# A second Strassen-like level for M3, and results added to the stored output by accumulating DMAs: an MLP block on one core

## The chip, the cores and the metric

One core of a Trainium2 chip runs the kernel. The metric is the device time in microseconds (us); a kernel's time is the median of several executions. The kernel before repeats within 0.25%.

## The reference, cut to what matters

```python
# x: 8 x 1024 x 1024, w1: 1024 x 4096, w2: 4096 x 1024, all float32
h = x @ w1
h = 0.5 * h * (1 + np.tanh(np.sqrt(2 / np.pi) * (h + 0.044715 * h ** 3)))
return (h @ w2).astype(np.float32)
```

## The kernel before

The kernel works in float16 and takes the 8192 rows in 8 superblocks (numbered from 0) of 1024 rows. Each matrix product is done in the manner of Strassen: the operands are cut into 2 x 2 blocks, and 7 products of sums of blocks replace 8. The first layer (`matmul1`) needs 448 matmuls of 128x512 for a superblock. The second layer (`matmul2`) has products M1 to M7, and its output has four blocks, "11", "12", "21" and "22".

A product at one level is 64 matmuls of 128x512 (13.81 us). A product listed in `INNER` is cut once more in the same manner: 112 matmuls of 128x256 (12.23 us), done by `inner_product`. That saves 1.58 us of TensorE, and costs seven loads of 512 KB in place of four, and more sums. M6 and M7 are inner from superblock 2 on, M1 from superblock 3 on.

A bank is one of the kernel's eight PSUM buffers (`pp`, `bufs=8`) in which TensorE leaves a result; u and d are float32 sums in SBUF, the on-chip memory, from which blocks "11" and "22" are stored; `w_d`, `raw_d` and `in_d` in the tables are operands in DRAM that SyncE loads. Pool is GpSimd.

The parts that matter here:

```python
INNER = (6, 7, 1)
...
up = ctx.enter_context(tc.tile_pool(name="up", bufs=26))   # operands, u and d
tp = ctx.enter_context(tc.tile_pool(name="tp", bufs=10))   # 128x512 float32 temporaries
...
def matmul1(xs, sb, quads):            # first layer: every hidden block takes temporaries
    ...
    for c in range(NI):
        ...
        product(pb, w, 4, True, False)
        v = temp()
        nc.scalar.copy(out=v, in_=pb)
        product(qb, w, 5, True, False)
        u = temp()
        tt(u, v, qb, SUB)              # VectorE
        ...
def matmul2(sb, g, next_x):            # second layer
    ...                                # M4 -> u, inner M1 added to u
    for q, ps in product(2, pb, False):
        c21[q] = temp()
        nc.scalar.copy(out=c21[q], in_=ps)
        store(sb, "21", q, c21[q])
    d2, d = halves()
    x6 = inner_x(6, g)
    xs = next_x()                      # SyncE transposes the next superblock's x
    for q, ps in product(5, qb, True):
        tt(u[q], u[q], ps, SUB)
        tt(d[q], u[q], c21[q], SUB)
    inner_product(6, x6, d2)           # M6 is added to d, in SBUF
    for q, ps in product(3, qb, False):
        c12 = temp()
        nc.scalar.copy(out=c12, in_=ps)
        store(sb, "12", q, c12)
        tt(d[q], d[q], ps, ADD)
        store(sb, "22", q, d[q])
    x7 = inner_x(7, g)
    ...                                # last superblock: results stored from SyncE
    inner_product(7, x7, u2)           # M7 is added to u, in SBUF
    for q in range(NQ):
        last = store(sb, "11", q, u[q])
```

The ten temporaries are shared by the second layer and the first layer of the next superblock. A temporary that is the source of a DMA is free again only when that DMA has landed.

Of the kernel before, what the change touches and what calls it, by code (L numbers as in the profile page):

```python
# [12 lines left out]
ADD = mybir.AluOpType.add  # L13
SUB = mybir.AluOpType.subtract
P = 128
# [32 lines left out]
SUMS = (4, 1, 3, 7, 6)  # L48
PLAIN = (2, 5)
# [3 lines left out]
    {(7, 2): 1, (7, 3): 1, (3, 0): 2, (3, 1): 3, (3, 2): 1, (3, 3): 2, (6, 0): 1, (6, 1): 1, (6, 2): 2, (6, 3): 5},  # L53
)

INNER = (6, 7, 1)
ORDER = (4, 5, 1, 2, 3, 7, 6)


# [1 line left out]
def kernel(  # L61
# [7 lines left out]
    nc = tc.nc  # L69
    x2 = x.flatten_outer_dims()  # L70
    out2 = out.flatten_outer_dims()
# [4 lines left out]
    SB = 1024  # L76
    HT = SB // 2
    NSB = T // SB
    KH = H // P // 2
    NI = I // P // 2  # L80
    OH = O // 2
    NQ = HT // P
# [18 lines left out]
    raw_d = [dram.tile([P, 4, KH * QW], DT, name=f"raw_d{q}") for q in range(NI // QC)]  # L101
    in_d = {m: dram.tile([P, 7, NI // 2, OH // 2], DT, name=f"in_d{m}") for m in INNER}
    w2_d = [dram.tile([P, 7, QC * OH], DT, name=f"w2_d{q}") for q in range(NI // QC)]
# [5 lines left out]
    def temp():  # L109
        return tp.tile([P, HT], F32, name="tmp")  # L110

    def unit(rows, cols):
        return up.tile([P, rows, cols], DT, name="u")

    def tt(out, in0, in1, op, pin=False):
        i = nc.vector.tensor_tensor(out=out, in0=in0, in1=in1, op=op)  # L116
        if pin:
            tc.keep_in_program_order(i)
# [272 lines left out]



    def store(sb, b, q, src):
        r0 = sb * SB + (int(b[0]) - 1) * HT + q * P
        o0 = (int(b[1]) - 1) * OH
        return nc.gpsimd.dma_start(out=out2[r0:r0 + P, o0:o0 + OH], in_=src)  # L397

    def matmul2_made(sb, g, keep_w1, xb):

# [37 lines left out]
        def add(m, q):  # L438
            u, op, v = B_TERMS[m]
            t = sums[m][q]  # L440
            tt(t, raw[u][q], raw[v][q], op, m != 4)
            if sb and m not in INNER[:2]:
                nc.gpsimd.dma_start(out=w2_d[q][:, m - 1, :], in_=flat(t))
# [97 lines left out]
    def split_inner(m, j, pieces):  # L541

        def block(k, b, h):
            return pieces[2 * k + h][:, :, b * OH // 2:(b + 1) * OH // 2]

        u, op, v = B_TERMS[j]
        d = in_d[m][:, j - 1]
        t = None if op is None else unit(NI // 2, OH // 2)
        for h in range(2):
            cs = slice(h * QC, (h + 1) * QC)  # L550
            x0 = block(int(u[0]) - 1, int(u[1]) - 1, h)
            if op is None:
                nc.gpsimd.dma_start(out=d[:, cs, :], in_=x0)
            else:
                tt(t[:, cs, :], x0, block(int(v[0]) - 1, int(v[1]) - 1, h), op, m != 1)
        if op is not None:
            nc.gpsimd.dma_start(out=d, in_=t)

    def inner_x(m, g):

        u, v = A_TERMS[m]
        x = {}
        for b in ("22", "12", "11", "21"):
            a, k = int(b[0]) - 1, int(b[1]) - 1
            at = (slice(None), slice(k * NI // 2, (k + 1) * NI // 2), slice(a * HT // 2, (a + 1) * HT // 2))
            x[b] = unit(NI // 2, HT // 2)
            tt(x[b], g[u][at], g[v][at], SUB)
        return x

    def inner_product(m, x, acc, done=lambda b, t: None):  # L570


        HK, HO = NI // 2, OH // 2
        y = {}
        for j in ORDER:
            y[j] = unit(HK, HO)
            nc.sync.dma_start(out=y[j], in_=in_d[m][:, j - 1])

        def product(j, bank, first):
            u, v = A_TERMS[j]  # L580
            if v is None:
                t = x[u]
            else:
                t = gcp.tile([P, HK, HT // 2], GT, name="gc")
                tt(t, x[u], x[v], SUB)
            for i in range(2):
                for c in range(HK):
                    nc.tensor.matmul(  # L588
                        bank[:, i * HO:(i + 1) * HO],
                        lhsT=t[:, c, i * P:(i + 1) * P],  # L590
                        rhs=y[j][:, c, :],
                        start=(first and i == 0 and c == 0),
                        stop=(c == HK - 1),
                        skip_group_check=not first or i > 0,
                    )

        def part(b):
            a, o = int(b[0]) - 1, int(b[1]) - 1
            return acc[a][:, :, o * HO:(o + 1) * HO]

        def pair(t):
            return t.rearrange("p (i n) -> p i n", i=2)

        pb, qb, rb = psum(), psum(), psum()
        product(4, pb, True)
        v = temp()
        nc.scalar.copy(out=v, in_=pb)
        product(5, qb, True)
        u = temp()
        tt(u, v, qb, SUB)  # L610
        nc.gpsimd.tensor_tensor(out=part("11"), in0=part("11"), in1=pair(u), op=ADD)  # L611
        product(1, rb, True)
        s = temp()
        tt(s, u, rb, ADD)
        product(2, pb, False)
        s2 = temp()
        tt(s2, s, pb, SUB)
        nc.gpsimd.tensor_tensor(out=part("22"), in0=part("22"), in1=pair(s2), op=ADD)

        def add(b, bank):  # L620
            tt(part(b), part(b), pair(bank), ADD)
            done(b, part(b))

        add("21", pb)
        product(3, qb, False)
        s3 = temp()
        nc.scalar.copy(out=s3, in_=qb)
        add("12", s3)
        product(7, rb, False)
        add("11", rb)  # L630
        product(6, qb, False)
        add("22", qb)

    def operand2(g, m, q, pin=False):

# [19 lines left out]
    def product2(g, m, pieces, banks, first, by_chunk=False):  # L655
        if first:
            banks.extend(psum() for _ in range(NQ))
        if by_chunk:
            for c0 in range(0, NI, QC):
                for q in range(NQ):  # L660
                    matmuls2(banks[q], operand2(g, m, q), pieces, first, range(c0, c0 + QC))
                    if c0 + QC == NI:
                        yield q, banks[q]
            return
        for q in range(NQ):
            matmuls2(banks[q], operand2(g, m, q), pieces, first)
            yield q, banks[q]

    def halves():
        tiles = [up.tile([P, 2, OH], F32, name="u") for _ in range(2)]  # L670
        return tiles, [tiles[q // 2][:, q % 2, :] for q in range(NQ)]

    def matmul2(sb, g, next_x):
        def load(m):
            return [load_ops(w2_d[q], raw2_d[q], (m,), QC, OH)[m] for q in range(NI // QC)]

        def product(m, banks, first):
            return product2(g, m, load(m), banks, first)

        c21 = {}  # L680
        pb, qb, rb = [], [], []
        p4 = product(4, pb, True)
        u2, u = halves()
        for q, ps in p4:
            nc.scalar.copy(out=u[q], in_=ps)
        if sb == 2:
            pieces = load(1)
            for q, ps in product2(g, 1, pieces, rb, True):
                tt(u[q], u[q], ps, ADD)
            for j in SUMS + PLAIN:  # L690
                split_inner(1, j, pieces)
        else:
            inner_product(1, inner_x(1, g), u2)
        for q, ps in product(2, pb, False):
            c21[q] = temp()
            nc.scalar.copy(out=c21[q], in_=ps)  # L696
            store(sb, "21", q, c21[q])
        d2, d = halves()
        x6 = inner_x(6, g)
        xs = next_x()  # L700
        for q, ps in product(5, qb, True):
            tt(u[q], u[q], ps, SUB)
            tt(d[q], u[q], c21[q], SUB)
        inner_product(6, x6, d2)
        for q, ps in product(3, qb, False):
            c12 = temp()
            nc.scalar.copy(out=c12, in_=ps)
            store(sb, "12", q, c12)
            tt(d[q], d[q], ps, ADD)
            store(sb, "22", q, d[q])  # L710
        x7 = inner_x(7, g)
        if sb == NSB - 1:

            def store_part(b, t):
                r0, o0 = sb * SB + (int(b[0]) - 1) * HT // 2, (int(b[1]) - 1) * OH // 2
                rows = out2[r0:r0 + HT // 2, o0:o0 + OH // 2]
                nc.sync.dma_start(out=rows.rearrange("(i p) n -> p i n", p=P), in_=t)

            inner_product(7, x7, u2, store_part)
            return None, xs  # L720
        inner_product(7, x7, u2)
        for q in range(NQ):
            last = store(sb, "11", q, u[q])
        return last, xs

    idle = consts.tile([P, HT], DT, name="idle")
    nc.vector.memset(idle, 0.0)
# [3 lines left out]
    xs, quads = x_first(), []  # L731
    for sb in range(NSB):
        g = matmul1(xs, sb, quads)
        if sb < 2:
            xb = x_cast(sb + 1, quads[2].stored) if sb else None
            last, xs, quads = matmul2_made(sb, g, None if sb else quads[-1].keep_raw, xb)
# [6 lines left out]
        last, xs = matmul2(sb, g, next_x)  # L743
# [33 lines left out]
```

## Time and profile before

| | before |
|---|---|
| time | 1548.62 us, median of 4 runs (1548.24 to 1548.99) |
| TensorE busy | 1537.9 of 1548.1 us, 8078 matmuls |
| TensorE waits, the four largest groups, whole run | 1.6, 1.5, 1.2 and 1.1 us |
| granted TensorE clock, mean | 1.00 |
| last matmul to end of the program | 3.9 us (1544.16 to 1548.1) |

The page of the profile, the kernel before: the busy time of each engine (PE is TensorE, PEld its weight load, DVE VectorE, ACT ScalarE, POOL GpSimd), with share of the span and number of instructions; then the DMA queue that Pool issues on (packets, MB, share of the time of all 16 DMA engines).

```profile
PE 1537.9 (99%) x8078; PEld 789.6 (51%) x8078; DVE 1036.4 (67%) x1294; ACT 486.1 (31%) x816; POOL 224.4 (14%) x311
...
q0 software_dynamic: 19440, 74.99, 14.7%
...
out_dram<-tmp POOLq DMA_DIRECT2D x72, 256.0 KB, 5.2
```

The last line is from the table of DMA issues: 72 stores of 256 KB from temporaries, 5.2 us from issue to landing in the median.

The chain of waits in order of time, the kernel before, last superblock (start, duration, engine, tile, line, count):

```profile
1355.52 96.69 PE ps L303 x448
1452.21 13.81 PE ps L646 x64
1466.02 12.23 PE ps L588 x112
1478.25 27.63 PE ps L646 x128
1505.88 12.23 PE ps L588 x112
1518.10 13.81 PE ps L646 x64
1531.92 12.24 PE ps L588 x112
1544.16 0.03 issue
```

This is one superblock read straight off: the first layer, M4, inner M1, M2 with M5, inner M6, M3, inner M7. Each line starts where the last one ended, so TensorE has no gap, and the time of the kernel is the time of its matmuls. Only fewer matmul cycles or new gaps can move it.

### The profile page before, as it was taken

To read this page: it belongs to the slowest core of one execution; us is meant where nothing else is said; L and a number is where in the kernel's file an instruction comes from. 1 tells how busy PE (TensorE), PEld (TensorE's weight loads), DVE (VectorE), ACT (ScalarE), POOL (GpSimd) and SP (SyncE) were. 2 spreads that over 40 slices of the span, in tenths; PEclk is the share of its full clock that TensorE was granted. 3 is DMA by queue.
4 is the path that set the end of the run, shared out by engine and by line. 5 is a ranking of instruction groups with operands and counts; after the bars stand their busy time and mean duration, and the time that the engine had idled before them with its cause. 6 is when DMAs were issued, how large, how long until landed. Compare 5 with 4: busy or idle time off the path is not lost.

```text
span 1548.1 us, 21098 instructions
## 1 busy us (share of the span) xinstructions
PE 1537.9 (99%) x8078; PEld 789.6 (51%) x8078; DVE 1036.4 (67%) x1294; ACT 486.1 (31%) x816; POOL 224.4 (14%) x311
## 2 busy tenths in 40 slices
PE   8999999999999999999999999999999999999998
PEld 4444444444444455445554456544565445744556
DVE  5876868758755666557665677656685567755575
ACT  6655024410244102441034410344113431144301
POOL 1242011112300013001130011200122001200012
PEclk9999999999999999999999999999999999999999
DMA  9999885894992869617795376944769357672553
GB/s 308 345 330 344 250 277 186 284 245 157 348 325 82 238 265 305 266 62 215 277 328 221 110 219 252 354 167 156 233 234 362 117 167 256 251 292 102 189 209 140
DMA packets 169156, 366.30 MB, mean 237 GB/s; under 512 B 73184, under 2 KB 80352, under 8 KB 168160
## 3 DMA queue, kind: packets, MB, share of 16 engines
q1 hardware_dynamic: 149616, 289.98, 54.4%
q0 software_dynamic: 19440, 74.99, 14.7%
q8 instruction: 63, 1.03, 0.3%
q14 instruction: 37, 0.30, 0.1%
HBM read 286.79 MB, written 92.80 MB: 245 GB/s over the span
## 4 chain that ended last, share of the span: by engine, by line
PE 96%; DMA 1%; DVE 1%; ACT 1%; issue 0%; SPq 0%; DVEq 0%; ACTq 0%
PE ps L303 48%; PE ps L646 35%; PE ps L588 13%; DMA gc<-in_w_dram 1%; DVE u L116 1%; DVE tmp L116 0%; ACT g L313 0%; SPq L126 0%; ACT u L191 0%; ACT u L153 0%; ACT u L265 0%; ACT tmp L363 0%; DVEq L116 0%; ACTq L153 0%
## 5 line engine op out<-in xcount | busy, mean ns | idle before, releaser
L303 PE MATMUL ps<-u 128*128 128x512 f16 x3584 | 776.4, 379 | 4.0 <-DVE tmp L116 1.6
L116 DVE TENSOR_TENSOR tmp<-tmp,ps 128x512 f32<-128x512 f32 x579 | 396.2, 686 | 348.6 <-ACT tmp L363 112.8
L303 PEld LDWEIGHTS <-u 128*128 128x128 f16 x3584 | 350.0, 98 | 428.2 <-issue 5.4
L646 PE MATMUL ps<-u,gc 128*128 128x512 f16 x1472 | 319.3, 379 | 0.0
L313 ACT ACTIVATE g<-tmp 128x512 f16<-128x512 f32 x256 | 161.2, 630 | 293.6 <-DVE tmp L116 293.5
L646 PEld LDWEIGHTS <-gc 128*128 128x128 f16 x1472 | 143.7, 98 | 172.9
L646 PE MATMUL ps<-u,g 128*128 128x512 f16 x1024 | 223.6, 379 | 0.0
L313 ACT ACTIVATE g<-ps 128x512 f16<-128x512 f32 x256 | 151.5, 596 | 90.5 <-PE ps L303 90.4
L116 DVE TENSOR_TENSOR u<-u 128x2048 f16<-128x2048 f16 (+2 forms) x164 | 166.1, 1049 | 17.5 <-ACT u L265 12.7
L646 PEld LDWEIGHTS <-g 128*128 128x128 f16 x1024 | 100.0, 98 | 119.7
L588 PE MATMUL ps<-u,gc 128*128 128x256 f16 x1360 | 154.0, 273 | 0.0
L588 PEld LDWEIGHTS <-gc 128*128 128x128 f16 x1360 | 132.9, 98 | 15.6
L116 DVE TENSOR_TENSOR u<-u,ps 128x512 f32<-128x512 f32 x119 | 81.3, 683 | 79.0 <-PE ps L646 47.6
L116 DVE TENSOR_TENSOR gc<-g,g 128x2048 f16<-128x2048 f16 x92 | 117.0, 1284 | 23.4 <-PE ps L646 22.0
L611 POOL TENSOR_TENSOR u<-u,tmp 128x512 f32<-128x512 f32 x17 | 37.0, 2177 | 641.7 <-DVE tmp L116 512.3
L116 DVE TENSOR_TENSOR gc<-u 128x2048 f16<-128x2048 f16 x85 | 101.2, 1217 | 0.0
L116 DVE TENSOR_TENSOR tmp<-ps,tmp 128x512 f32<-128x512 f32 x128 | 88.3, 690 | 6.2 <-PE ps L303 1.2
L363 ACT COPY tmp<-ps 128x512 f32<-128x512 f32 x128 | 72.9, 569 | 52.2 <-PE ps L303 52.1
L116 DVE TENSOR_TENSOR u<-g,g 128x2048 f16<-128x2048 f16 x68 | 79.5, 1216 | 3.5 <-ACT g L313 3.5
L397 POOL DMA_DIRECT2D out_dram<-tmp x72 | 39.4, 548 | 264.9 <-ACT tmp L696 85.9
L588 PE MATMUL ps<-u 128*128 128x256 f16 x544 | 64.9, 273 | 0.0
L588 PEld LDWEIGHTS <-u 128*128 128x128 f16 x544 | 53.1, 98 | 9.9
(35 smaller groups left out, 331.1 us busy)
## 6 DMA issues: line engine op xcount, KB each, us to landing
u<-w_d SPq DMA_DIRECT2D x172, 512.0 KB, 10.1
u<-raw_d SPq DMA_DIRECT2D x128, 512.0 KB, 8.7
u<-in_d SPq DMA_DIRECT2D x119, 512.0 KB, 6.4
gc<-in_w_dram SPq DMA_DIRECT2D x48, 512.0 KB, 6.0
out_dram<-tmp POOLq DMA_DIRECT2D x72, 256.0 KB, 5.2
raw_d<-u SPq DMA_DIRECT2D x32, 512.0 KB, 9.9
w_d<-u POOLq DMA_DIRECT2D x32, 512.0 KB, 4.4
xb<-in_x_dram POOLq DMA_DIRECT2D x56, 256.0 KB, 11.4
```

The lines of the kernel that those rows point to most:

```text
L116: i = nc.vector.tensor_tensor(out=out, in0=in0, in1=in1, op=op)
L303: nc.tensor.matmul(bank, lhsT=ops[m][:, k, cs], rhs=xs[m][:, k, :], start=(first and k == 0), stop=(k == KH - 1), skip_group_check=not first,)
L313: gelu_last[0] = nc.scalar.activation(out=g[b][:, c, :], in_=src, func=GELU)
L363: nc.scalar.copy(out=v, in_=pb)
L397: return nc.gpsimd.dma_start(out=out2[r0:r0 + P, o0:o0 + OH], in_=src)
L588: nc.tensor.matmul(bank[:, i * HO:(i + 1) * HO], lhsT=t[:, c, i * P:(i + 1) * P], rhs=y[j][:, c, :], start=(first and i == 0 and c == 0), ...
L611: nc.gpsimd.tensor_tensor(out=part("11"), in0=part("11"), in1=pair(u), op=ADD)
L646: nc.tensor.matmul(bank, lhsT=a[:, c, :], rhs=pieces[c // QC][:, c % QC, :], start=(first and c == 0), stop=(c == NI - 1), skip_group_chec ...
```

## The change

The intent: M3 also becomes an inner product from superblock 3 on, 1.58 us less of TensorE in each of five superblocks. Before, M3's matmuls went on adding in the banks that held M5 (block "12" is M3 + M5); an inner M3 can't, so the order and the way of adding change too: M3 comes before M5, M3's blocks are stored at once, and M5, M6 and M7 are added to what already stands in the output in DRAM, by DMAs that accumulate. The kernel issues these DMAs from Pool.

The diff, cut to its core:

```diff
-INNER = (6, 7, 1)
+INNER = (6, 7, 1, 3)
...
+    def store_quarter(sb, o, b, src, add=True):
+        r0 = sb * SB + (int(o[0]) - 1) * HT + (int(b[0]) - 1) * HT // 2
+        o0 = (int(o[1]) - 1) * OH + (int(b[1]) - 1) * OH // 2
+        rows = out2[r0:r0 + HT // 2, o0:o0 + OH // 2].rearrange("(i p) n -> p i n", p=P)
+        return nc.gpsimd.dma_start(out=rows, in_=src, **(dict(accum_op=ADD) if add else {}))
...  # inner_product: with acc=None each quarter of the result stays in a temporary and goes to done()
...  # matmul2, after M4, inner M1 and M2:
+        if sb == 2:
+            for q, ps in plain(3, []):      # M3 at one level; writes M3's inner operands
+                c12 = temp()
+                nc.scalar.copy(out=c12, in_=ps)
+                store(sb, "12", q, c12)
+                tt(d[q], d[q], ps, ADD)
+                store(sb, "22", q, d[q])
+        else:
+
+            def done3(b, t):
+                store_quarter(sb, "12", b, pair(t), False)
+                tt(quarter(d2, b), quarter(d2, b), pair(t), ADD)
+                store_quarter(sb, "22", b, quarter(d2, b), False)
+
+            inner_product(3, inner_x(3, g), done3)
         x6 = inner_x(6, g)
         xs = next_x()
         for q, ps in product(5, qb, True):
+            c5 = temp()
+            nc.scalar.copy(out=c5, in_=ps)
+            store(sb, "12", q, c5, accum_op=ADD)
             tt(u[q], u[q], ps, SUB)
-            tt(d[q], u[q], c21[q], SUB)
-        inner_product(6, x6, d2)
...  # M3 and the last superblock's stores from SyncE were here
-        inner_product(7, x7, u2)
-        for q in range(NQ):
-            last = store(sb, "11", q, u[q])
-        return last, xs
+            store(sb, "11", q, u[q])
         x7 = inner_x(7, g)
+        inner_product(6, x6, lambda b, t: store_quarter(sb, "22", b, pair(t)))
+        last = []
+        inner_product(7, x7, lambda b, t: last.append(store_quarter(sb, "11", b, pair(t))))
+        return last[-1], xs
```

More of the change, by code (lines that the diff above doesn't have):

```diff
@@ L390, in matmul1, with store @@
         return g
-    def store(sb, b, q, src):
+    def store(sb, b, q, src, **kw):
         r0 = sb * SB + (int(b[0]) - 1) * HT + q * P
         o0 = (int(b[1]) - 1) * OH
-        return nc.gpsimd.dma_start(out=out2[r0:r0 + P, o0:o0 + OH], in_=src)
+        return nc.gpsimd.dma_start(out=out2[r0:r0 + P, o0:o0 + OH], in_=src, **kw)
+    def store_quarter(sb, o, b, src, add=True):
[3 more added lines that the diff above has]
+        return nc.gpsimd.dma_start(out=rows, in_=src, **(dict(accum_op=ADD) if add else {}))
     def matmul2_made(sb, g, keep_w1, xb):
@@ L554, in split_inner @@
             else:
-                tt(t[:, cs, :], x0, block(int(v[0]) - 1, int(v[1]) - 1, h), op, m != 1)
+                tt(t[:, cs, :], x0, block(int(v[0]) - 1, int(v[1]) - 1, h), op, m in INNER[:2])
         if op is not None:
@@ L565, in inner_x @@
             at = (slice(None), slice(k * NI // 2, (k + 1) * NI // 2), slice(a * HT // 2, (a + 1) * HT // 2))
+            if v is None:
+                x[b] = g[u][at]
+                continue
             x[b] = unit(NI // 2, HT // 2)
@@ L568, in inner_x, with quarter, pair, inner_product @@
         return x
-    def inner_product(m, x, acc, done=lambda b, t: None):
+    def quarter(acc, b):
+        a, o = int(b[0]) - 1, int(b[1]) - 1
+        return acc[a][:, :, o * OH // 2:(o + 1) * OH // 2]
+    def pair(t):
+        return t.rearrange("p (i n) -> p i n", i=2)
+    def inner_product(m, x, done, acc=None):
         HK, HO = NI // 2, OH // 2
@@ L595, in product, with copied, whole, add @@
                     )
-        def part(b):
-            a, o = int(b[0]) - 1, int(b[1]) - 1
-            return acc[a][:, :, o * HO:(o + 1) * HO]
-        def pair(t):
-            return t.rearrange("p (i n) -> p i n", i=2)
+        def copied(bank):
+            t = temp()
+            nc.scalar.copy(out=t, in_=bank)
+            return t
+        def whole(b, t):
+            if acc is not None:
+                tt(quarter(acc, b), quarter(acc, b), pair(t), ADD)
+            done(b, t)
+        def add(b, bank, t):
+            if acc is None:
+                tt(t, t, bank, ADD)
+                done(b, t)
+            else:
+                tt(quarter(acc, b), quarter(acc, b), pair(bank), ADD)
+        def early(b, t):
+            if acc is not None:
+                nc.gpsimd.tensor_tensor(out=quarter(acc, b), in0=quarter(acc, b), in1=pair(t), op=ADD)
         pb, qb, rb = psum(), psum(), psum()
         product(4, pb, True)
-        v = temp()
-        nc.scalar.copy(out=v, in_=pb)
+        v = copied(pb)
         product(5, qb, True)
@@ L610, in inner_product @@
         tt(u, v, qb, SUB)
-        nc.gpsimd.tensor_tensor(out=part("11"), in0=part("11"), in1=pair(u), op=ADD)
+        early("11", u)
         product(1, rb, True)
@@ L615, in inner_product @@
         product(2, pb, False)
-        s2 = temp()
+        s2 = s if acc is None else temp()
         tt(s2, s, pb, SUB)
-        nc.gpsimd.tensor_tensor(out=part("22"), in0=part("22"), in1=pair(s2), op=ADD)
-        def add(b, bank):
-            tt(part(b), part(b), pair(bank), ADD)
-            done(b, part(b))
-        add("21", pb)
+        early("22", s2)
+        whole("21", copied(pb))
         product(3, qb, False)
-        s3 = temp()
-        nc.scalar.copy(out=s3, in_=qb)
-        add("12", s3)
+        whole("12", copied(qb))
         product(7, rb, False)
-        add("11", rb)
+        add("11", rb, u)
         product(6, qb, False)
-        add("22", qb)
+        add("22", qb, s2)
     def operand2(g, m, q, pin=False):
@@ L678, in product @@
             return product2(g, m, load(m), banks, first)
-        c21 = {}
         pb, qb, rb = [], [], []
@@ L685, in matmul2, with plain @@
             nc.scalar.copy(out=u[q], in_=ps)
+        def plain(m, banks):
+            pieces = load(m)
+            yield from product2(g, m, pieces, banks, True)
+            for j in SUMS + PLAIN:
+                split_inner(m, j, pieces)
         if sb == 2:
-            pieces = load(1)
-            for q, ps in product2(g, 1, pieces, rb, True):
+            for q, ps in plain(1, rb):
                 tt(u[q], u[q], ps, ADD)
-            for j in SUMS + PLAIN:
-                split_inner(1, j, pieces)
-        else:
-            inner_product(1, inner_x(1, g), u2)
+        else:
+            inner_product(1, inner_x(1, g), lambda b, t: None, u2)
+        d2, d = halves()
         for q, ps in product(2, pb, False):
-            c21[q] = temp()
-            nc.scalar.copy(out=c21[q], in_=ps)
-            store(sb, "21", q, c21[q])
-        d2, d = halves()
+            c21 = temp()
+            nc.scalar.copy(out=c21, in_=ps)
+            store(sb, "21", q, c21)
+            tt(d[q], u[q], c21, SUB)
+        if sb == 2:
[5 more added lines that the diff above has]
+                store(sb, "22", q, d[q])
+        else:
+            def done3(b, t):
[3 more added lines that the diff above has]
+            inner_product(3, inner_x(3, g), done3)
         x6 = inner_x(6, g)
@@ L701, in matmul2 @@
         for q, ps in product(5, qb, True):
+            c5 = temp()
+            nc.scalar.copy(out=c5, in_=ps)
+            store(sb, "12", q, c5, accum_op=ADD)
             tt(u[q], u[q], ps, SUB)
-            tt(d[q], u[q], c21[q], SUB)
-        inner_product(6, x6, d2)
-        for q, ps in product(3, qb, False):
-            c12 = temp()
-            nc.scalar.copy(out=c12, in_=ps)
-            store(sb, "12", q, c12)
-            tt(d[q], d[q], ps, ADD)
-            store(sb, "22", q, d[q])
-        x7 = inner_x(7, g)
-        if sb == NSB - 1:
-            def store_part(b, t):
-                r0, o0 = sb * SB + (int(b[0]) - 1) * HT // 2, (int(b[1]) - 1) * OH // 2
-                rows = out2[r0:r0 + HT // 2, o0:o0 + OH // 2]
-                nc.sync.dma_start(out=rows.rearrange("(i p) n -> p i n", p=P), in_=t)
-            inner_product(7, x7, u2, store_part)
-            return None, xs
-        inner_product(7, x7, u2)
-        for q in range(NQ):
-            last = store(sb, "11", q, u[q])
-        return last, xs
+            store(sb, "11", q, u[q])
+        x7 = inner_x(7, g)
+        inner_product(6, x6, lambda b, t: store_quarter(sb, "22", b, pair(t)))
+        last = []
+        inner_product(7, x7, lambda b, t: last.append(store_quarter(sb, "11", b, pair(t))))
+        return last[-1], xs
     idle = consts.tile([P, HT], DT, name="idle")
```

## The prediction

> What bounds the kernel now. TensorE does. It is busy 1537.9 of 1548.1 us (page, busy times), and in the chain of waits in order of time it runs without any gap from 70 us to 1544.16 us. From superblock 3 on a superblock is 96.7 us of first-layer matmuls, then M4 13.81, inner M1 12.23, M2+M5 27.63, inner M6 12.23, M3 13.81, inner M7 12.23. Clock 1.00 throughout. Only fewer matmul cycles or new TensorE gaps can move the time.
>
> Removed. M3 at the second level is 112 matmuls of 128x256 (12.23 us) instead of 64 of 128x512 (13.81 us): 1.58 us for each of superblocks 3 to 7, 7.9 us in all, and all of it on the critical path. Pool's and VectorE's adds into u and d for M6 and M7 go too, off the path.
>
> Added. (1) M3 needs 7 loads of 512 KB instead of 4, plus superblock 2 writes M3's seven inner operands. (2) Out blocks 12, 22, 11 are written twice, the second time by accumulating DMAs[...]. The trace has no accumulate, so its speed is unknown; plain 256 KB stores here take 5.2 to 6.6 us to land (page, DMA issues), up to 12.9.
>
> Moved, and here I expect the loss. In the instruction order of the changed kernel, VectorE's last add of inner M3 (s2 + the bank of product 6, which waits for M3's last matmul) stands in front of the first operand subtraction of M5, and M5's first weight load waits for that. [...] In the old order no product waited for the end of an inner one. Cost, from the trace: 0.09 us from TensorE's last matmul to VectorE, 0.60 until the next operation can start behind a 128x512 add, 1.22 for the 128x2048 subtraction[...]: 2.2 us in each of five superblocks, about 11 us. That alone is more than the 7.9 saved. (TensorE's clock should hold[...].)
>
> Second, M7's third operand load now waits on SyncE for the stores of u (issued some 13 us after M5's start, landing 6 to 12 later), and six loads of M7 and the next superblock's seven w1 loads queue behind it. That window already ran DMA at 1.0 share and 381 GB/s before. I expect some TensorE gaps around inner M7 and the start of the next superblock, 0 to 4 us each, about 6 us in sum.
>
> Third, the end: the last result goes out by an accumulating DMA from Pool instead of SyncE's (2.1 us to landing): about +2 us.
>
> Sum: 1548.7 - 7.9 + 11 + 6 + 2 = about 1559 us, range 1548 to 1575. Chances: faster by over 2% 0.01, within 2% 0.92, slower by over 2% 0.07.
>
> Right if: TensorE matmul count rises by 5 x 48 = 240; inner M3 takes 12.2 us; TensorE idles about 2.2 us just before M5 in superblocks 3 to 7, released by a VectorE subtraction; the last matmul ends later than 1544 us. Wrong if: that gap is missing (then 1541 to 1546), or accumulates land so slowly (over 12 us) that temporary buffers and loads run out and each superblock loses 5 us or more (then beyond 1575).

The gap before M5: the sum for that gap came to 2.2 us; the three terms, all from the trace, come to 1.91 us, and the rest was the author's estimate. The 11 us in the forecast of 1559 are five times 2.2.

## The result, and the profile after

| | before | after |
|---|---|---|
| time, median of 4 runs | 1548.62 us | 1633.51 us (1625.63 to 1636.33) |
| ratio after / before | | 1.054, 95% interval 1.0503 to 1.0577 |
| span of the profiled run | 1548.1 | 1634.6 |
| matmuls | 8078 | 8318 |
| mean granted clock | 1.00 | 0.976 |

The kernel became 5.4% slower. Ratios in this document are the mean time of one kernel's runs over that of the other's runs of the same rounds, so they are not quite the ratio of the medians beside them.

The page of the profile, the kernel after, the same lines as before:

```profile
PE 1553.1 (95%) x8318; PEld 819.0 (50%) x8318; DVE 1068.8 (65%) x1330; ACT 504.8 (31%) x852; POOL 280.7 (17%) x372
...
q0 software_dynamic: 37312, 98.59, 22.5%
...
out_dram<-tmp POOLq DMA_DIRECT2D x144, 256.0 KB, 7.2
```

There are 240 more matmuls, as the change intends (5 x 48). But TensorE is busy 15.2 us longer for 7.9 us less work, so about 23 us of its busy time comes from a lower clock; and it's idle for 81.5 us of the span where it was idle for 10.2, 71 us more. Stores from temporaries doubled in number and land later.

The waits of TensorE, the kernel after (engine, tile and line that waited, releaser, us in total, times, longest):

```profile
PE ps L303 <- DVE tmp L116: 42.9, 12, 6.7
PE ps L668 <- DVE gc L116: 15.6, 5, 3.1
PE ps L668 <- DMA u<-raw_d: 9.7, 3, 8.6
```

These three lines hold nearly all the new idle time. L303 is the first layer; L668 is a one-level second-layer product, here M5.

The timeline of TensorE around one superblock change, the kernel after (start, duration, what ran; in brackets the idle time before it and what ended it):

```profile
921.90 13.98 PE L668 MATMUL ps<-u,g 128*128 128x512 f16 x64
...
977.27 15.60 PE L668 MATMUL ps<-u,gc 128*128 128x512 f16 x64 [3.12 <-DVE gc L116]
...
1017.16 9.66 PE L303 MATMUL ps<-u 128*128 128x512 f16 x44
1028.40 1.02 PE L303 MATMUL ps<-u 128*128 128x512 f16 x4 [1.58 <-DVE tmp L116]
1036.08 89.40 PE L303 MATMUL ps<-u 128*128 128x512 f16 x400 [6.66 <-DVE tmp L116]
```

M5 starts after a gap of 3.12 us and takes 15.60 us (mean granted clock 0.89 from 977.27 to 992.90); M4, without a gap before it, takes 13.98 in the same view. What stands before M5 on VectorE, whose subtraction makes M5's first weights (timeline of VectorE; M3's last matmul ends at 974.15):

```profile
975.40 0.68 DVE L116 TENSOR_TENSOR tmp<-tmp,ps 128x512 f32<-128x512 f32 x1
976.00 1.22 DVE L116 TENSOR_TENSOR gc<-g,g 128x2048 f16<-128x2048 f16 x1
```

Then the first layer runs for 44 matmuls and stops twice, 8.2 us in all. What holds it is VectorE (`DVE tmp`), and the timeline of VectorE says what holds VectorE:

```profile
1023.84 0.69 DVE L116 TENSOR_TENSOR tmp<-tmp,ps 128x512 f32<-128x512 f32 x1 [1.72 <-DMA out_dram<-tmp]
1027.66 0.69 DVE L116 TENSOR_TENSOR tmp<-tmp,ps 128x512 f32<-128x512 f32 x1 [3.13 <-DMA out_dram<-tmp]
1031.62 0.69 DVE L116 TENSOR_TENSOR tmp<-ps,tmp 128x512 f32<-128x512 f32 x1 [3.27 <-DMA out_dram<-tmp]
```

Each add writes a new temporary, and each has to wait until a store from an older temporary has landed. In these lines a temporary came free only every 3.8 to 4.0 us. Over the whole run VectorE waits 67.1 us for this, 25 times (the waits of all engines: `DVE tmp L116 <- DMA out_dram<-tmp`); before, there is no such wait of VectorE at all. One of these landings stands in the chain of waits of the kernel after, at another superblock change:

```profile
1422.65 18.53 DMA out_dram<-tmp
```

That accumulate took 18.53 us from its issue to its landing. The quarter stores of L403 as a whole (88, of which 48 accumulate), from issue to landing, in the kernel after and then in e1 below, where the same 88 are all plain:

```profile
DMA to landing us min/median/max: 4.2/9.0/20.8
```

```profile
DMA to landing us min/median/max: 2.5/7.1/9.9
```

The table of stretches, the kernel after, same superblock (busy time of each engine, then granted TensorE clock, DMA share and GB/s):

```profile
1017.16:1027.00 9.84, 9.66 (x46) 4.31 (x44) 3.43 (x5) 3.00 (x5) 4.48 (x7) 1.00 1.11 324
1027.00:1036.08 9.08, 1.02 (x4) 0.38 (x4) 2.06 (x3) 1.60 (x3) 1.46 (x3) 0.76 1.11 324
1036.08:1042.00 5.92, 5.92 (x14) 2.02 (x14) 1.91 (x3) 1.10 (x2) 0.49 (x1) 0.50 1.14 287
```

The same view before, at the same stage, the first 12 us of a first layer:

```profile
978.26:990.00 11.74, 11.74 (x57) 5.31 (x55) 6.66 (x10) 4.71 (x8) 5.43 (x11) 1.00 1.07 380
```

The DMA engines are a little busier (1.11 to 1.14 against 1.07; the share adds up the times of all packets, so it can pass 1) and move less (287 to 324 GB/s against 380). And after the gaps TensorE runs at half clock (0.50 from 1036.08 to 1042.00).

**How slow is an accumulate?** The clearest place is the end of the program, where nothing else moves. The DMA view, a window of 21 us from 1615 us on, the kernel after (40 slices of 0.53 us: busy share of the DMA engines in tenths, and GB/s; then the packets of the queue and their share of 16 engines' time):

```profile
DMA  9999994000000008699999999999981000000000
GB/s 127 187 164 125 135 164 76 12 4 0 0 0 0 0 0 31 57 187 185 113 113 172 160 70 144 187 131 140 162 129 16 0 0 0 0 0 0 0 0 0
...
q0 software_dynamic: 1616, 1.55, 58.9%
```

The same view of a window of 14 us from 1536 us on, the kernel before (slices of 0.35 us), whose last stores are plain ones from SyncE with rows of 1 KB, the same quarter blocks:

```profile
DMA  0000000000000019900099179400794000000000
GB/s 12 23 0 0 0 0 0 0 0 0 0 0 0 0 61 357 319 12 0 18 334 348 50 269 342 138 0 0 269 348 132 0 0 0 0 0 0 0 0 0
...
q1 hardware_dynamic: 1088, 1.05, 22.0%
```

At a busy share of 9 tenths the accumulates move 70 to 187 GB/s, the plain stores 319 to 357. Per packet: 58.9% of 16 engines x 21 us, over 1616 packets, is 122 ns; 22.0% of 16 x 14 us, over 1088 packets, is 45 ns. Both kinds have packets of 1 KB, so here it isn't the packet size; but the queues differ, Pool's and SyncE's. Run e9 below settles that: it stores the same quarter blocks plain from Pool, and in a window of 16 us from 1534 on its queue takes 18.9% of 16 engines for 1.06 MB, 46 us of engine time per MB. SyncE's took 47, the accumulates 128. The trace's packet records for the whole run say the same of the Pool queue: M6's and M7's accumulates are 12288 packets of 1024 B at 106 ns in the mean, M5's are 3072 packets of 2048 B at 200 ns, and plain stores are packets of 4096 B at 177 ns. Per byte the two accumulating kinds cost nearly the same, and 2.3 to 2.4 times what a plain store costs (2.7 at the end of the program). All accumulates together took 120 us of all 16 engines; at the plain rate it would be about 51 (an estimate from these numbers).

### Where the 86.5 us of the profiled spans are

| part | us | read from |
|---|---|---|
| M3 at two levels, 5 x 1.58 | -7.9 | chain before, 12.23 against 13.81 |
| first-layer gaps, 42.9 - 1.6 | +41.3 | waits of TensorE |
| gaps before M5, 5 x 3.12 | +15.6 | waits of TensorE |
| gap in M5 of superblock 2 | +9.7 | waits of TensorE |
| half clock after those gaps | +22.1 | the rest; busy time says 15.2 + 7.9 = 23.1 |
| last matmul to end, 9.6 - 3.9 | +5.7 | timelines: last matmul ends 1625.0 and 1544.16 |
| sum | +86.5 | 1634.6 - 1548.1 |

The clock's line is what is left over, so the sum closes by construction; the busy time is a check of it, 1 us apart.

### The profile page after: what moved, and what is told of

It is laid out like the page before. It is cut to its first block, busy times and chain, and to the rows that moved or that the text cites. A ratio compares the mean times of both kernels' runs of the same rounds, so it can differ in the third digit from the quotient of the medians. Undisturbed runs are those within 1.5% of the kernel's fastest.

```text
span 1634.6 us, 21893 instructions
## 1 busy us (share of the span) xinstructions
PE 1553.1 (95%) x8318; PEld 819.0 (50%) x8318; DVE 1068.8 (65%) x1330; ACT 504.8 (31%) x852; POOL 280.7 (17%) x372
## 3 DMA queue, kind: packets, MB, share of 16 engines
q0 software_dynamic: 37312, 98.59, 22.5%
q8 instruction: 65, 1.06, 0.3%
## 5 line engine op out<-in xcount | busy, mean ns | idle before, releaser
L303 PE MATMUL ps<-u 128*128 128x512 f16 x3584 | 786.9, 382 | 44.4 <-DVE tmp L116 42.9
L116 DVE TENSOR_TENSOR tmp<-tmp,ps 128x512 f32<-128x512 f32 x628 | 429.7, 685 | 408.6 <-ACT tmp L363 104.0
L303 PEld LDWEIGHTS <-u 128*128 128x128 f16 x3584 | 352.8, 98 | 476.3 <-issue 60.3
L668 PE MATMUL ps<-u,gc 128*128 128x512 f16 x1472 | 332.0, 388 | 25.3 <-DVE gc L116 15.6
L668 PEld LDWEIGHTS <-gc 128*128 128x128 f16 x1472 | 146.3, 100 | 207.3 <-issue 25.4
L604 PE MATMUL ps<-u,gc 128*128 128x256 f16 x1760 | 199.3, 273 | 0.0
L604 PEld LDWEIGHTS <-gc 128*128 128x128 f16 x1760 | 172.3, 98 | 19.9
L116 DVE TENSOR_TENSOR u<-u 128x2048 f16<-128x2048 f16 (+2 forms) x174 | 170.7, 1017 | 17.2 <-ACT u L265 12.5
L668 PE MATMUL ps<-u,g 128*128 128x512 f16 x704 | 153.7, 379 | 0.0
L116 DVE TENSOR_TENSOR gc<-g,g 128x2048 f16<-128x2048 f16 x92 | 112.8, 1242 | 9.5 <-PE ps L668 8.1
L116 DVE TENSOR_TENSOR gc<-u 128x2048 f16<-128x2048 f16 x85 | 102.2, 1218 | 23.8 <-PE ps L668 23.8
L632 POOL TENSOR_TENSOR u<-u,tmp 128x512 f32<-128x512 f32 x10 | 21.5, 2147 | 543.7 <-DVE tmp L116 440.9
L668 PEld LDWEIGHTS <-g 128*128 128x128 f16 x704 | 68.9, 98 | 83.1
L116 DVE TENSOR_TENSOR tmp<-ps,tmp 128x512 f32<-128x512 f32 x128 | 88.3, 690 | 22.3 <-DMA out_dram<-tmp 16.1
L403 POOL DMA_DIRECT2D out_dram<-tmp x68 | 72.1, 1175 | 130.8 <-ACT tmp L615 120.9
L615 ACT COPY tmp<-ps 128x512 f32<-128x512 f32 x66 | 37.2, 588 | 181.6 <-DVE tmp L116 127.1
L397 POOL DMA_DIRECT2D out_dram<-tmp x76 | 49.8, 656 | 240.5 <-ACT tmp L722 90.5
L363 ACT COPY tmp<-ps 128x512 f32<-128x512 f32 x128 | 73.0, 570 | 55.4 <-PE ps L303 55.4
L116 DVE TENSOR_TENSOR u<-g,g 128x2048 f16<-128x2048 f16 x68 | 79.6, 1217 | 3.5 <-DMA u<-in_d 2.8
```

The lines of the kernel that those rows point to most:

```text
L116: i = nc.vector.tensor_tensor(out=out, in0=in0, in1=in1, op=op)
L303: nc.tensor.matmul(bank, lhsT=ops[m][:, k, cs], rhs=xs[m][:, k, :], start=(first and k == 0), stop=(k == KH - 1), skip_group_check=not first,)
L397: return nc.gpsimd.dma_start(out=out2[r0:r0 + P, o0:o0 + OH], in_=src, **kw)
L403: return nc.gpsimd.dma_start(out=rows, in_=src, **(dict(accum_op=ADD) if add else {}))
L604: nc.tensor.matmul(bank[:, i * HO:(i + 1) * HO], lhsT=t[:, c, i * P:(i + 1) * P], rhs=y[j][:, c, :], start=(first and i == 0 and c == 0), ...
L615: nc.scalar.copy(out=t, in_=bank)
```

## The experiments

Eleven kernels were run, in three rounds on three chips, each round with its own runs of the kernel before (shared medians 1548.68, 1548.74 and 1548.76 us). Unless said otherwise the result was correct.

The theory: accumulating DMAs are slow, they hold the temporaries, and the next first layer stops for want of one. The rivals: M3's extra loads and the double writing fill the DMA, whether accumulating or not; or the new order of instructions does it.

### e1: the same stores, without accumulating

```diff
-        return nc.gpsimd.dma_start(out=rows, in_=src, **(dict(accum_op=ADD) if add else {}))
+        return nc.gpsimd.dma_start(out=rows, in_=src, **{})
...
-            store(sb, "12", q, c5, accum_op=ADD)
+            store(sb, "12", q, c5)
```

The result is wrong (nothing is added to the stored output; relative error 0.90). Bytes and order are as in the kernel after; the packets aren't: the queue has 26560 in place of 37312, because the plain stores go in packets of 4096 B.

> The changed kernel with every accumulating DMA made a plain one of the same shape (wrong result on purpose). Theory A, accumulates land late and hold the 10 temporary buffers: the 8 us of gaps at the start of each first layer from superblock 3 on vanish (below 1 us each) and the end shrinks by 5 us, while the 3.1 us gap before M5 stays: about 1577 us. Rival B, M3's extra loads fill the DMA engines and any store would land late: those gaps stay at 5 us or more, over 1610 us.

Measured: 1580.9 us (1577.24 to 1582.61), ratio 1.0206. The waits of TensorE and the Pool queue:

```profile
PE ps L668 <- DVE gc L116: 15.6, 5, 3.1
PE ps L668 <- DMA u<-raw_d: 5.8, 4, 4.4
PE ps L303 <- DVE tmp L116: 1.8, 2, 1.5
...
q0 software_dynamic: 26560, 98.59, 18.7%
```

The first-layer waits fall from 42.9 to 1.8 us, while the queue carries the same 98.59 MB. Its engine time falls from 22.5% of 1634.6 to 18.7% of 1575.5 us, 368 to 295 us: 73 us of DMA time were the accumulating, with its smaller packets. So of 85 us lost, 52.6 go when accumulating goes, against the rival of mere traffic. They are not all first-layer gaps: in the profiled runs, 59.1 us apart, the first-layer waits are 41.1 us less, the stall in superblock 2 is 3.9 less and the end 2.1 less (9.6 to 7.5, where 5 less was expected); most of the rest is half clock. The gaps before M5 stay as they were, to a tenth: they have another cause.

### e2: M3 at one level, accumulates kept

```diff
-INNER = (6, 7, 1, 3)
+INNER = (6, 7, 1)
...
-        if sb == 2:
-            for q, ps in plain(3, []):
+        if True:
+            for q, ps in product(3, [], True):
```

> The accumulating DMAs alone: M3 stays one-level in all superblocks, everything else as changed. Theory A: first-layer gaps stay near 8 us each, the gap before M5 and superblock 2's stall go: 1634 + 8 - 24 - 11 = about 1607 us. Rival B (M3's second level is the harm): first-layer gaps under 2 us, at most 1565 us.

Measured: 1600.7 us (1599.95 to 1601.43), ratio 1.0337.

```profile
PE ps L303 <- DVE tmp L116: 39.6, 11, 7.0
PE ps L303 <- DVE u L116: 1.5, 1, 1.5
```

The first-layer gaps are as long without M3's extra loads. The gaps before M5 and the one in superblock 2 are gone. So the change's two halves fail apart: adding by DMA costs the first-layer gaps, the second level of M3 brings the others.

### e3 and e6: M6 and M7, or M7 alone, added on chip again

```diff
 # e6: M7 only
-            store(sb, "11", q, u[q])
...
-        inner_product(7, x7, lambda b, t: last.append(store_quarter(sb, "11", b, pair(t))))
+        inner_product(7, x7, lambda b, t: None, u2)
+        for q in range(NQ):
+            last.append(store(sb, "11", q, u[q]))
```

e3 does the same to M6 with d, and drops the early stores of block "22".

> M3 two-level and M5 by accumulating DMA as changed, but M6 and M7 added to d and u on chip as before and stored once, plain. Theory A: first-layer gaps gone, end as before (4 us after the last matmul), gap before M5 stays: about 1575 us. Rival B: over 1600 us. Rival C (VectorE has no room for the adds): new gaps inside M6 or M7 released by VectorE, over 1590 us.

> Only M7 is added to u on chip and stored plain; M6 and M5 stay accumulating DMAs. M6's four accumulates are issued 12 us earlier than M7's, so held buffers are back before the first layer wants them: first-layer gaps under 2 us, about 1585 to 1595 us, close to M6 and M7 both on chip (1587.7). If the total of accumulating traffic decides, half of the loss stays: about 1610 us.

Measured: e3 1587.7 us (1582.19 to 1589.63), ratio 1.0247; e6 1579.6 us (1576.65 to 1582.72), ratio 1.0197. In both the first-layer gaps are gone: the waits of the first layer for temporaries are 1.2 us in e3 and 1.3 in e6. e6 came out 5 us below its range; e3 was expected some 12 us faster than it came out. It had a new wait, five times:

```profile
PE ps L604 <- ACT tmp L615: 7.3, 5, 1.5
```

In M7 TensorE stands 1.45 us until a ScalarE copy has emptied a bank into a temporary. The trace shows the copy waiting for VectorE (at 995.63 us, after `8.51 <-DVE tmp L116`), and VectorE without idle time from 976.1 us until then, with sums for M7's operands and M6's adds queued up: rival C in part. e7 below takes the copy out. The gaps before M5 stay in e3, but after two of the five M5 runs at full clock, as here:

```profile
958.50 13.99 PE L668 MATMUL ps<-u,gc 128*128 128x512 f16 x64 [3.12 <-DVE gc L116]
```

e6 shows that M7 is the product that counts. Its four accumulates are the last before the next first layer. M6's and M5's still accumulate in e6, and VectorE still waits 11.8 us for temporaries in the whole run, but that no longer reaches TensorE.

### e4: M5's first operands made early

```diff
         product(6, qb, False)
+        ahead()                   # M3 only: M5's first two operand subtractions, pinned
         add("22", qb, s2)
```

> The changed kernel with M5's first two operand subtractions placed before M3's last adds on VectorE. The order theory: the 3.1 us gap before M5 goes in superblocks 3 to 7 and with it the 1.65 us that M5 loses to the throttled clock: 1634 - 24 = about 1610 us, first-layer gaps unchanged near 8 us. Rival: the gap is a wait for M5's loads, and stays: within 5 us of 1634.

Measured: 1612.4 us (1611.94 to 1612.81), ratio 1.0413. The five gaps before M5 are gone, and M5 starts without a wait and runs at full clock:

```profile
969.14 13.98 PE L669 MATMUL ps<-u,gc 128*128 128x512 f16 x64
```

The gaps held 15.6 us and the half clock in M5 another 8 (M5's durations). The 21 us gained are a net sum: the first layer's waits fall too, from 44 to 34 us, which was not expected, while the inner products get 3.5 us of new waits and half clock appears elsewhere (the mean granted clock is still 0.985). e4 also shows where the gap came from. In the kernel after, the subtraction that M5's first weights need ran at 976.00 us, behind an add at 975.40 that waits for M3's last matmul (timeline of VectorE above); placed before that add, it leaves no gap. In the first layer, waits for the w1 loads now take the place of part of the waits for temporaries (17.6 us for temporaries, 13.6 for loads).

### e5: one more temporary

```diff
-    tp = ctx.enter_context(tc.tile_pool(name="tp", bufs=10))
+    tp = ctx.enter_context(tc.tile_pool(name="tp", bufs=11))
```

> The changed kernel with 11 temporary buffers instead of 10. VectorE gets its buffers back one accumulate at a time, about 3.8 us apart (trace). If it is the held buffers that stop the first layer, one more buffer saves about one such step: first-layer gaps 8 to about 4 us, 5 x 4 = 20 us less, about 1614 us. If the stop is a matter of DMA traffic alone, nothing changes: within 5 us of 1634.

Measured: 1619.9 us (1617.36 to 1623.01), ratio 1.0461. The waits of TensorE:

```profile
PE ps L303 <- DVE tmp L116: 19.9, 10, 4.5
```

One buffer of 2 KB per partition is worth 14 us, 2.7 for each superblock change. That is the direct test of the claim that temporaries run out, and it holds in direction. It's less than the 20 expected, because the freed time is partly taken by other waits (TensorE waits 7.5 us for ScalarE's copies into temporaries in the first layer, and 2.5 us for w1 loads). A kernel with twelve doesn't build: the temporaries would need 24 KB of each partition, and by the builder's message 23.84 KB are left.

### e7 and e8: the second level of M3 without the rest

e7 combines e3 and e4, adds M6's and M7's quarters to d and u straight from the banks (which takes out e3's late copy), and stores the last superblock from SyncE as before. e8 is e7 with M3's second level from superblock 4 on instead of 3, its operands being written in superblock 3 and not in 2.

```diff
 # e7, in inner_product
-        whole("21", copied(pb))
+        if acc is None:
+            whole("21", copied(pb))
+        else:
+            add("21", pb, None)
 # e8, over e7
-        if sb == 2:
-            for q, ps in plain(3, []):
+        if sb in (2, 3):
+            for q, ps in (plain(3, []) if sb == 3 else product(3, [], True)):
```

> M3 two-level and M5 by accumulating DMA as changed; M6 and M7 on chip straight from the banks as before; M5's first two operands early; last results stored from SyncE as before. All gaps but superblock 2's (5 to 10 us and a throttled clock) should be gone: 1548.7 - 7.9 + 8 to 13 = 1549 to 1554 us.

> The same, with M3 one-level and split in superblock 3, not 2, so superblock 2 is as before: the gain is 4 x 1.58 = 6.3 us less small gaps: 1543 to 1547 us, faster than before by 0.1 to 0.4%. If superblock 3 then has superblock 2's trouble: 1550 to 1555.

Measured: e7 1553.6 us (1552.44 to 1555.59, 5 runs), ratio 1.0032, interval 1.002 to 1.0045. e8 1544.9 us (1543.9 to 1545.56, 5 runs), ratio 0.9975, interval 0.9963 to 0.9988. The waits of TensorE in e7 and in e8:

```profile
PE ps L673 <- DMA u<-raw_d: 8.1, 3, 6.4
PE ps L604 <- DVE tmp L116: 2.5, 4, 0.6
```

```profile
PE ps L604 <- DVE tmp L116: 1.9, 3, 0.6
PE ps L303 <- DVE tmp L116: 1.6, 2, 1.4
```

e8 is the only version here whose interval lies below the kernel before: 3.9 us by the medians. Four superblocks with two-level M3 save 6.3 us; three gaps of 0.62 us in M7 take 1.9 back. In both, M5 is still added by accumulating DMAs, with no wait to be seen. e7's profile differs from e8's by the stall in superblock 2, 8.1 us.

### e11: the stall of superblock 2

In superblock 2 SyncE first issues the next superblock's 16 transposes, then M5's loads. The timeline of SyncE, the kernel after:

```profile
531.99 25.78 SPq L288 DMA_TRANSPOSE u<-xb  x16
557.88 2.80 SPq L212 DMA_DIRECT2D u<-raw_d  x4
```

M5 should have started at about 561, and its first loads were issued at 558. In the kernel before the transposes started at 506.66, M5's loads were issued at 530.64, and M5 began some 18 us later. Before the late transposes SyncE stands 21.3 us until VectorE releases it (`SPq L288 <- DVE u L116: 21.3, 1, 21.3`, waits of SyncE); in e11 below M5's loads come first, and they wait there 21.1 us in place of the transposes. A shortage of operand buffers, since M3's four loads now come before the transposes, would fit this but was not tested. e11 is e7 with M5's loads put first:

```diff
         x6 = inner_x(6, g)
+        w5 = load(5)
         xs = next_x()
-        for q, ps in product2(g, 5, load(5), qb, True, made=made5):
+        for q, ps in product2(g, 5, w5, qb, True, made=made5):
```

> The version with M3 at the second level from superblock 3 (1553.6 us), with M5's loads in superblock 2 issued before the next superblock's transposes. If only the order on SyncE made the 6.4 us wait there: it goes and nothing replaces it, about 1545 us. If the operand buffers or the DMA time of superblock 2 are short (splitting M3 writes seven more 512 KB operands there): the wait moves to a later product or to the next first layer, about 1551 to 1555 us.

Measured: 1544.8 us median, four runs at 1543.49, 1544.69, 1544.94 and 1551.54; ratio 0.999, interval 0.9967 to 1.0012. M5's wait is gone in the profile, and what comes in its place is 1.7 us in all, for M6's loads. So with the late start as it is, the order on SyncE makes the stall. One run in four was slow, without a profile, and why isn't known; therefore e8, whose five runs lie within 1.7 us, is the better version of the two.

### e9: the last stores from Pool instead of SyncE

```diff
 # the kernel before, store_part of the last superblock
-                nc.sync.dma_start(out=rows.rearrange("(i p) n -> p i n", p=P), in_=t)
+                nc.gpsimd.dma_start(out=rows.rearrange("(i p) n -> p i n", p=P), in_=t)
```

> The kernel before, with only the last superblock's result stores issued from Pool instead of SyncE (plain stores, no accumulate). Theory: the stretch from the end of the last matmul to the end of the span was 3.9 us with SyncE's stores, 9.2 us with plain Pool stores in the run without accumulates and 11.4 us in the changed kernel, so issuing from Pool by itself costs about 5.3 us: expect about 1554 us, last matmul still near 1544. Rival: the long end belongs to the queue being full of earlier stores in the changed kernel; then here within 1 us of before, 1548.7.

Measured: 1549.9 us (1549.48 to 1550.29), ratio 1.0008, interval 0.9993 to 1.0023, so the times don't tell the two kernels apart. The expectation missed. It also rested on a misreading: the chain of waits had left out the last 16 matmuls of the kernel after and of e1, so the ends that it quotes, 11.4 and 9.2 us, are really 9.6 and 7.5 us by the timeline of TensorE. By one profile of each, issuing from Pool costs about 1.5 us of the end (5.4 us from the last matmul at 1542.3 to 1547.7, against 3.9), not 5.3. In the kernel after the DMA engines work on until 1631.0, at the low rate shown above, so the accumulates are another part. Between there and 1634.6 the profile shows no transfer of data; what fills those 3.6 us (1.3 us before, 2.1 in e9, 4.2 in e1) was not found out.

### e10: M6 by accumulating DMAs, in the fast version

```diff
 # over e8
-        inner_product(6, x6, lambda b, t: None, d2)
-        for q in range(NQ):
-            store(sb, "22", q, d[q])
+        inner_product(6, x6, lambda b, t: store_quarter(sb, "22", b, pair(t)))
```

The early stores of block "22" come back with it.

> The faster version (M6 and M7 on chip, M5's operands early, M3 plain in superblocks 2 and 3), with M6 alone back on accumulating DMAs, M7 on chip. Theory: temporaries run short only where accumulates of M6 and M7 follow one another with the next superblock's w1 and operand loads; M6 alone (24 accumulates of 256 KB in all) should do no harm: 1543 to 1547 us, no TensorE wait above 2 us. Rival: any accumulate with rows of 1 KB slows the DMA enough to make waits: above 1555.

Measured: 1561.9 us (1559.41 to 1564.44), ratio 1.0085 where e8 has 0.9975, so about 17 us slower than e8. The theory's number missed here. The waits of TensorE:

```profile
PE ps L303 <- DMA u<-w_d: 9.2, 7, 4.8
PE ps L303 <- DMA u<-raw_d: 2.4, 2, 1.3
...
PE ps L604 <- DMA u<-in_d: 1.3, 3, 0.7
```

These are waits for loads, not for temporaries, and the timeline puts nearly all of them into one place, the end of superblock 3 and the first layer after it (774 to 811 us). There M3's operands are being written as well, and even e8 had the DMA engines at a share of 1.03 to 1.05 from 749 to 811 us, without a TensorE gap. So accumulates had two prices here. They hold their source for longer (quarter stores landed after 9.0 us in the median in the kernel after, 7.1 in e1), and they take DMA time that the loads need (per byte 2.3 to 2.4 times a plain store's in the kernel after); which one showed was a matter of what was short at that place. The time lies in the rival's range (above 1555), but the rival, that any such accumulate makes waits, isn't borne out either: in the other superblocks of e10 the waits come to about 1 us or less.

## Why the prediction was wrong, and where it was right

1. *What bounds the kernel* was right. TensorE without gaps was the whole time, and all that was lost came in as gaps, the clock after them, and the end.
2. *Removed, 7.9 us* was right. There are 240 more matmuls, inner M3 takes the 12.2 us of an inner product, and e8 turns four fifths of it (6.3 us) into time, less 1.9 us of small gaps.
3. *The gap before M5* was right in its place, its number (five), its releaser and its cause (e4 removes it). Its size was not: 3.12 us, not 2.2. The sum of 2.2 took VectorE to be idle when M3 ends. The 0.09 us from M3's last matmul to VectorE's add were 1.25 (974.15 to 975.40). In the trace VectorE has no idle time from 965.5 to 977 us: subtractions of 1.2 us for M6's operands and adds into d and temporaries were queued up, so the add behind M3's last matmul and then M5's subtraction (976.00 us) came late.
4. *TensorE's clock should hold* was wrong. No trace showed the reason given for it; the trace before couldn't test it, as its longest wait of TensorE is 1.5 us. The trace after shows M5 taking 15.48 to 15.67 us instead of 13.98 after each of the five gaps of 3.12, so they cost 4.7 us each, 24 in all, where the prediction had 11. Not every such gap was followed by half clock: after 5 of the 15 in e1, e3 and e5 M5 took 13.99 us (a line of e3 is shown above).
5. *"0 to 4 us each, about 6 us in sum"* around inner M7 and the next first layer is the step that failed. It was looked for in the loads that queue behind the stores of u. What the runs showed is another mechanism: accumulates of the temporaries, landing up to 18.5 us after issue in the chain of waits, so that the first layer has none to write into. It cost 41 us of gaps and about 10 of half clock after them (the five stretches of 400 matmuls took 442 us; at the rate of 448 in 96.69 they would take 432), some 50 us in all. e1's 52.6 us agree, less the shorter stall and end noted there; e1, e2, e5 and e6 show it from four sides. The prediction had put beside it only the plain stores, "5.2 to 6.6 us to land", because the trace before has no accumulate. Its own list of what would make it wrong named this case, with the right consequence (each superblock loses 5 us or more, beyond 1575); it gave a result slower by over 2% a chance of 0.07.
6. *The stall of superblock 2*, 9.7 us and the clock after it, was not foreseen at all. The prediction had noted the seven operands written there as bytes, and hadn't asked when SyncE would come to M5's loads. e11 shows that putting them first is enough to end it; why SyncE came so late stays open.
7. *The end, +2 us* was too small; it was +5.7. About 1.5 of it is Pool's issuing by e9. The slow accumulates are another part that was only read from the DMA view, and some of it stays open.

## What to carry to other kernels

An accumulating DMA is not a store with a free add: it took 2.3 to 2.7 times the DMA time of a plain store per byte here, and its source buffer stays taken for longer (quarter stores landed after 9.0 us in the median and 20.8 at most, against 7.1 and 9.9 when all were plain), so count the buffers in flight at the place where the next stage asks for them. Where TensorE is the limit and VectorE has room, add on chip (with M7 alone added so, the first layer's waits for temporaries fell from 42.9 to 1.3 us), and check in the order of each engine's queue that no operand of the next product stands behind an add that waits for the last one. A saving of 1.58 us for a product is smaller than one gap of 3.12 us, and 20 of the 25 such gaps here were paid again in the clock.

## What was measured of the clock and of accumulating DMAs

- In the kernel after, e1, e3, e5 and e6, M5 stands behind 25 gaps of 3.12 to 3.13 us. After 20 of them its 64 matmuls took 15.28 to 16.91 us, after 5 of them 13.99 (timelines of TensorE; 13.98 without a gap). After a gap of 2.42 us in e5, 20 matmuls took 6.16 us; after one of 3.60 us in e4, 20 took 4.48. Gaps of 0.62 us in e8 left the mean clock at 1.00. So the gap's length alone did not decide; what does was not shown.
- In the kernel after, accumulating packets took 106 ns for 1 KB and 200 ns for 2 KB, against 177 ns for 4 KB of plain stores on the same queue.
- In the kernel after, Pool took 1.19 us to issue an accumulate of 256 KB in quarter rows, 0.71 us for the same store without accumulating, and 0.54 us for a plain store of a whole 128x512 tile.
- The buffer that an accumulate reads from was the shortage. The ten temporaries ran out, and the first layer lost about 8 us at each of five superblock changes (41.3 us more than before, in all).
